# MLP matmuls with both activation parts side by side: one 512-column matmul in place of two of 256

## The chip, the cores and the metric

The kernel runs on one core of a Trainium2 chip. The metric is the device time of one execution in microseconds (us). Three runs of the kernel before gave 954.02, 955.78 and 957.56 us, median 955.78.

## The reference, cut to what matters

The reference is a small network on 256 tokens of width 1024 in float32: two transformer layers (attention, then an MLP), then an mLSTM mixer, an attention mixer with compressed and selected blocks, and a last norm. The change touches the two MLPs:

```python
def squared_relu_mlp(h, w_up, w_down):                 # w_up 1024 x 4096, w_down 4096 x 1024
    u = jnp.einsum("bsd,df->bsf", h, w_up)
    return jnp.einsum("bsf,fd->bsd", jnp.square(jax.nn.relu(u)), w_down)

h = rms_norm(x, g_mlp[layer])
x = x + squared_relu_mlp(h, w_up[layer], w_down[layer])
```

The norm's factor per token is taken out of the square: the kernel multiplies un-normed activations and scales the sum at the end.

## The kernel before, in words

Activations lie feature-major: a tile has 128 features on the partitions and the 256 tokens (`T`) as columns. Every matmul operand is cut into a high part (rounded to the reduced format `fp32r`) and a low part (what is left), and a product is the sum of three matmuls: high weights by high activations, high weights by low activations, low weights by high activations. The low-by-low product is left out.

Weights come as some 140 chunks of 128 x 2048 values, one DMA each on SyncE's queue (`prepare`, L120). ScalarE cuts the high part of a chunk in two halves (`whi`, L117), VectorE subtracts for the low part (`wlo`, L118). The ring has three buffers each of `wraw`, `whi` and `wlo`, so a chunk's buffers come free when TensorE has finished the chunk three before it.

`bank_add` (L189) issues, for every block of 128 input features and each of two output tiles (`j`), the three matmuls of 256 columns (L197, L199, L200), each with its own weight load. `gemm_feat` (L202) does that for one chunk: 8 blocks x 2 tiles x 3 = 48 matmuls into one PSUM bank (2 tiles x 256 columns). `gemm_tok` (L155) is the other form, used outside the MLPs: there the activations are the stationary operand and the weights stream, 512 columns at a time (L171 to L173).

`mlp` (L306): in the up part 16 chunks run, each giving 2 feature tiles of the hidden layer. ScalarE takes relu out of PSUM, VectorE squares, and both cut the square into `hh` and `hl` (`split`, L139). In the down part 4 groups of 4 chunks run; each group fills one bank, and `residual` (L278) scales it by the token's factor (`res`, L283), adds it to the stream `xT` (L285), and writes the next stage's operands `xh` (ScalarE, L237) and `xl` (VectorE, L238) and the squares for the norm. The two MLPs stand at about 116 to 287 us and 413 to 595 us of the span; the first is followed by `layer1`, whose first matmuls are of the 512-column form, the second by `mlstm`, whose first are `gemm_feat` chunks in an order written out by hand.

PSUM has eight banks: three for matmul outputs named `g`, two named `s` (attention scores, spare outputs), two `t`, one `o`. A scheduler orders each engine's instructions, mostly in the order of the program, and may pull a later chunk's matmuls forward where the next one would wait.

Of the kernel before, what the change touches and what calls it, by code (L numbers as in the profile page):

```python
# [8 lines left out]
F32 = mybir.dt.float32  # L9
F32R = mybir.dt.float32r  # L10
I32 = mybir.dt.int32
AF = mybir.ActivationFunctionType
ALU = mybir.AluOpType
# [3 lines left out]
P = 128  # L17
T = 256
KT = 8
# [48 lines left out]
def late(pool, shape, name):  # L68

    n = int(np.prod(shape))  # L70
    t = pool.tile([P, SHIFT + n], F32R, name=name, tag=name, bufs=1, align_bytes=LINE)[:, SHIFT:]
    names = "abcdefg"[:len(shape)]
    return t.rearrange(f"p ({' '.join(names)}) -> p {' '.join(names)}", **dict(zip(names, shape)))


class Builder:
# [229 lines left out]
    def mlp(self, gi_next):  # L306
        nc, tc = self.nc, self.tc
        with tc.tile_pool(name="mlp", bufs=2) as pool:
            hh = late(pool, [32, T], "hh")
            hl = late(pool, [32, T], "hl")  # L310
            for n in range(16):
                ps = self.gemm_feat()
                r = pool.tile([P, 2, T], F32, name="relu", tag="relu")
                s = pool.tile([P, 2, T], F32, name="rsq", tag="rsq")
                nc.scalar.activation(r, ps, AF.Relu)
                nc.vector.tensor_tensor(s, r, r, op=ALU.mult)
                self.split(hh[:, 2 * n:2 * n + 2], hl[:, 2 * n:2 * n + 2], s)
            self.norm_end("recip")
            row = self.rstd_row()
            if gi_next == 4:  # L320
                self.mlstm_fold()
            for n in range(4):
                b = self.bank()
                for c in range(4):
                    acts = [(hh[:, 8 * c + k], hl[:, 8 * c + k]) for k in range(8)]
                    self.bank_add(b, self.chunk(), 0, acts, c == 3)
                self.residual(2 * n, b["ps"], gi_next, row)


    def tok_evac(self, pool, ps, tag, sq=None, width=512, bufs=1):  # L330
# [805 lines left out]
    def build(self):  # L1136
        nc, tc = self.nc, self.tc
        with tc.tile_pool(name="keep", bufs=1) as keep, \
                tc.tile_pool(name="ring", bufs=3) as self.ring, \
                tc.tile_pool(name="small", bufs=2) as self.small, \  # L1140
                tc.tile_pool(name="pg", bufs=3, space=bass.MemoryType.PSUM) as self.pg, \
                tc.tile_pool(name="pa", bufs=1, space=bass.MemoryType.PSUM) as self.pa:
            self.vec = keep.tile([P, VEC.n], F32, name="vec", tag="vec")
            self.cst = keep.tile([P, CST.n], F32, name="cst", tag="cst")
            self.xT = keep.tile([P, KT, T], F32, name="xT", tag="xT")
            self.xh = late(keep, [KT, T], "xh")
            self.xl = late(keep, [KT, T], "xl")
            self.G = keep.tile([P, 16, 4], F32, name="G", tag="G")
            self.W8 = keep.tile([P, 2, 16, 8], F32, name="W8", tag="W8")
            self.ones = keep.tile([P, 1], F32, name="ones", tag="ones")  # L1150
            self.selr = keep.tile([P, 16], F32R, name="selr", tag="selr")
            nc.vector.memset(self.ones, 1.0)
            warm = keep.tile([P, 1], F32, name="warm", tag="warm")
            nc.scalar.activation(warm, self.ones, AF.Exp)
            self.ident = CST(self.cst, "ident")
            self.begin()
            self.pr = None
            with tc.tile_pool(name="p0", bufs=1, space=bass.MemoryType.PSUM) as self.p0:
                self.layer0()
            with tc.tile_pool(name="pr", bufs=2, space=bass.MemoryType.PSUM) as self.pr:  # L1160
                for s in (lambda: self.mlp(2), self.layer1, lambda: self.mlp(4), self.mlstm, self.nsa):
                    s()
# [146 lines left out]
```

## Time and profile before

| | |
|---|---|
| runs of the kernel before | 954.02, 955.78, 957.56 us (median 955.78) |
| the profiled execution's own time | 956.5 us |
| its span (first to last instruction) | 954.6 us |
| TensorE matmul busy | 936.7 us (98%) |
| weight load busy | 857.0 us (90%) |
| VectorE busy, ScalarE busy | 701.5 us (73%), 566.5 us (59%) |
| granted TensorE clock, mean | 0.997 |

Matmuls are pipelined: one row of a matmul lasts 0.28 us though the next begins 0.11 us later. So the pace of a stream of matmuls is read from the starts, or from how many stand in a stretch, not from the duration of one. A count in a stretch holds every matmul that touches it.

### The profile page before, as it was taken

The page shows a single profiled execution, that of the slowest core. Times are in us where ns is not written, and L with a number is a line of the kernel's source. Part 1 is how long each engine was busy: PE and PEld are TensorE (multiplying, and loading weights), DVE is VectorE, ACT ScalarE, POOL GpSimd, SP SyncE. Part 2 cuts the span into 40 slices and gives each one's busy share as a digit, 9 for nine tenths or more (in the row PEclk, how much of TensorE's full clock was granted, in tenths as well). Part 3 has the DMA queues.
Part 4 walks back from the last instruction along what each step waited for, and adds up shares of the span by engine and source line. Part 5 has one row for each costly group of instructions (what it writes and reads, how often), then busy time and mean ns, then how long its engine had stood idle before and what let it go on. Part 6 is the DMA issues. An engine that isn't in the chain of part 4 may idle for free.

```text
span 954.6 us, 17609 instructions
## 1 busy us (share of the span) xinstructions
PE 936.7 (98%) x7080; PEld 857.0 (90%) x7080; DVE 701.5 (73%) x1523; ACT 566.5 (59%) x1043; POOL 6.8 (1%) x16
## 2 busy tenths in 40 slices
PE   8998999999999999999999999999999999999997
PEld 5777899999998878899999999999888998988986
DVE  6788876664556887997665555978688877678994
ACT  7675665644435786765554344555755466379883
POOL 0000000000000000000000000000000000000000
PEclk9999999999999999999999999999999999999998
DMA  8823265555655333265555555544312555351311
GB/s 296 343 89 133 89 221 182 208 185 189 209 179 182 128 133 133 76 232 186 197 192 177 180 185 201 183 170 144 133 49 85 177 191 177 133 176 46 111 46 45
DMA packets 22610, 152.52 MB, mean 160 GB/s; under 512 B 2608, under 2 KB 2736, under 8 KB 4992
## 3 DMA queue, kind: packets, MB, share of 16 engines
q1 hardware_dynamic: 21744, 148.40, 45.1%
q0 software_dynamic: 784, 2.98, 0.9%
q8 instruction: 56, 0.92, 0.4%
q14 instruction: 26, 0.21, 0.1%
HBM read 150.33 MB, written 1.05 MB: 159 GB/s over the span
## 4 chain that ended last, share of the span: by engine, by line
PE 87%; ACT 5%; DVE 5%; issue 1%; DMA 1%; SPq 0%; ACTq 0%; DVEq 0%
PE g L197 19%; PE g L199 19%; PE g L200 18%; PE g L171 4%; PE g L173 4%; PE g L172 4%; PE o L475 2%; PE t L439 2%; DVE wlo L118 2%; ACT whi L117 2%; PE s L1043 1%; PE s L172 1%; PE s L171 1%; PE s L173 1%; PE t L366 1%; PE s L925 1%
## 5 line engine op out<-in xcount | busy, mean ns | idle before, releaser
L118 DVE TENSOR_TENSOR wlo<-wraw,whi 128x1024 fp32r<-128x1024 f32 (+1 forms) x274 | 325.3, 1204 | 143.9 <-ACT whi L117 143.4
L117 ACT ACTIVATE whi<-wraw 128x1024 fp32r<-128x1024 f32 (+1 forms) x274 | 277.5, 1042 | 228.8 <-PE g L199 121.8
L200 PE MATMUL g<-xh,wlo 128*128 128x256 f32 x928 | 261.4, 282 | 0.0
L199 PE MATMUL g<-xl,whi 128*128 128x256 f32 x928 | 260.4, 281 | 0.8 <-DVE xl L238 0.8
L197 PE MATMUL g<-xh,whi 128*128 128x256 f32 x928 | 260.5, 281 | 0.0
L197 PEld LDWEIGHTS g<-xh,whi 128*128 128x128 f32 x928 | 174.3, 188 | 3.7 <-issue 2.6
L199 PEld LDWEIGHTS g<-xl,whi 128*128 128x128 f32 x928 | 174.7, 188 | 1.5 <-DVE xl L238 1.2
L200 PEld LDWEIGHTS g<-xh,wlo 128*128 128x128 f32 x928 | 175.6, 189 | 0.5
L200 PE MATMUL g<-hh,wlo 128*128 128x256 f32 x512 | 142.9, 279 | 0.0
L197 PE MATMUL g<-hh,whi 128*128 128x256 f32 x512 | 142.9, 279 | 0.0
L199 PE MATMUL g<-hl,whi 128*128 128x256 f32 x512 | 142.8, 279 | 0.0
L199 PEld LDWEIGHTS g<-hl,whi 128*128 128x128 f32 x512 | 97.3, 190 | 0.0
L197 PEld LDWEIGHTS g<-hh,whi 128*128 128x128 f32 x512 | 96.2, 188 | 0.0
L200 PEld LDWEIGHTS g<-hh,wlo 128*128 128x128 f32 x512 | 96.2, 188 | 0.0
L171 PE MATMUL g<-whi,xh 128*128 128x512 f32 (+1 forms) x192 | 75.1, 391 | 0.9 <-ACT xh L237 0.9
L173 PE MATMUL g<-whi,xl 128*128 128x512 f32 (+1 forms) x192 | 74.2, 388 | 0.0
L172 PE MATMUL g<-wlo,xh 128*128 128x512 f32 (+1 forms) x192 | 74.0, 385 | 0.0
L197 PE MATMUL g<-yh,whi 128*128 128x256 f32 x224 | 62.7, 283 | 0.5 <-ACT yh L140 0.5
L199 PE MATMUL g<-yl,whi 128*128 128x256 f32 x224 | 62.6, 281 | 0.1
L200 PE MATMUL g<-yh,wlo 128*128 128x256 f32 x224 | 62.2, 280 | 0.0
L412 ACT ACTIVATE L<-L,nm 128x128 f32<-128x128 f32 (+1 forms) x128 | 56.9, 449 | 8.0 <-DVE nm L409 7.8
L171 PEld LDWEIGHTS g<-whi,xh 128*128 128x128 f32 x192 | 36.3, 189 | 10.6 <-ACT xh L237 2.9
(357 smaller groups left out, 1418.6 us busy)
## 6 DMA issues: line engine op xcount, KB each, us to landing
wraw<-in_w SPq DMA_DIRECT2D x135, 1024.0 KB, 5.0
wraw<-in_w SPq DMA_DIRECT2D x4, 512.0 KB, 7.8
tabs<-in_tabs SPq DMA_DIRECT2D x2, 1024.0 KB, 8.2
xT<-in_x SPq DMA_DIRECT2D x4, 256.0 KB, 7.9
bdv<-in_bdv POOLq DMA_DIRECT2D x8, 128.0 KB, 4.7
mlw<-in_mlw POOLq DMA_DIRECT2D x1, 992.0 KB, 5.2
nq<-in_gf POOLq DMA_DIRECT2D x1, 512.0 KB, 3.7
out_y<-nqr SPq DMA_DIRECT2D x2, 256.0 KB, 2.1
```

The costliest lines, as they stand in the source:

```text
L117: self.nc.scalar.activation(hi[:, s], w[:, s], AF.Copy)
L118: self.nc.vector.tensor_tensor(lo[:, s], w[:, s], hi[:, s].bitcast(F32), op=ALU.subtract)
L171: nc.tensor.matmul(ps[b][:, :n], xh, hi[:, sl], start=kt == 0, stop=False)
L172: nc.tensor.matmul(ps[b][:, :n], xh, lo[:, sl], start=False, stop=False)
L173: nc.tensor.matmul(ps[b][:, :n], xl, hi[:, sl], start=False, stop=kt == KT - 1)
L197: nc.tensor.matmul(o, hi[:, s], ah, start=bank["new"], stop=False)
L199: nc.tensor.matmul(o, hi[:, s], al, start=False, stop=False)
L200: nc.tensor.matmul(o, lo[:, s], ah, start=False, stop=last and j == 1 and i == len(acts) - 1)
L366: nc.tensor.transpose(ps[:, i, b * P:(b + 1) * P], t[:, b, c0 + i * P:c0 + (i + 1) * P], self.ident)
L412: nc.scalar.activation(Ls[i][:, c], Ls[i][:, c], AF.Exp, bias=nm[:, b, i:i + 1], scale=-1.0, accum_out=den[:, b, i:i + 1])
L439: nc.tensor.transpose(ps[:, e, j * P:(j + 1) * P], Ls[e][:, i * P:(i + 1) * P], self.ident)
L475: nc.tensor.matmul(o[64 * e:64 * e + 64, kt * P:T], v[:, kt, c0[e]:c0[e] + 64], pts[kt][:, e], start=start and kt == 0, stop=stop and kt == 1)
```

## The change

The low part of an activation is laid right behind its high part: `xx[:, k]` holds `xh` and `xl` of block `k` as 512 columns, `hx[:, f]` the same for the hidden layer. For each block and output tile there are now two matmuls in place of three: high weights by both parts (512 columns, one whole bank), and low weights by the high part (256 columns, the bank's first half). Each output tile has its own bank, one `g` and one `s`; the bank's two halves are added at the end by a ScalarE copy and a VectorE add per tile. Relu and square become one VectorE instruction on the sum.

```diff
-            hh = late(pool, [32, T], "hh")
-            hl = late(pool, [32, T], "hl")
+            hx = late(pool, [32, 2, T], "hx")
             for n in range(16):
-                ps = self.gemm_feat()
-                r = pool.tile([P, 2, T], F32, name="relu", tag="relu")
+                banks = self.wide()
+                self.wide_add(banks, self.chunk(), [self.xx[:, k] for k in range(8)], True, True)
+                u = self.wide_sum(pool, banks)
                 s = pool.tile([P, 2, T], F32, name="rsq", tag="rsq")
-                nc.scalar.activation(r, ps, AF.Relu)
-                nc.vector.tensor_tensor(s, r, r, op=ALU.mult)
-                self.split(hh[:, 2 * n:2 * n + 2], hl[:, 2 * n:2 * n + 2], s)
+                nc.vector.scalar_tensor_tensor(s, u, 0.0, u, op0=ALU.max, op1=ALU.mult)
+                self.split(hx[:, 2 * n:2 * n + 2, 0], hx[:, 2 * n:2 * n + 2, 1], s)
...
             for n in range(4):
-                b = self.bank()
+                banks = self.wide()
                 for c in range(4):
-                    acts = [(hh[:, 8 * c + k], hl[:, 8 * c + k]) for k in range(8)]
-                    self.bank_add(b, self.chunk(), 0, acts, c == 3)
-                self.residual(2 * n, b["ps"], gi_next, row)
+                    self.wide_add(banks, self.chunk(), [hx[:, 8 * c + k] for k in range(8)], c == 0, c == 3)
+                self.residual(2 * n, self.wide_sum(pool, banks), gi_next, row)
+
+    def wide(self):
+        return [self.pg.tile([P, 2, T], F32, name="g", tag="g"), self.single("s", [P, 2, T])]
+
+    def wide_add(self, banks, w, acts, first, last):
+        nc = self.nc
+        hi, lo = w
+        for i, a in enumerate(acts):
+            for j in range(2):
+                s = slice((2 * i + j) * P, (2 * i + j + 1) * P)
+                nc.tensor.matmul(banks[j], hi[:, s], a, start=first and i == 0, stop=False)
+                nc.tensor.matmul(banks[j][:, 0], lo[:, s], a[:, 0], start=False, stop=last and i == len(acts) - 1)
+
+    def wide_sum(self, pool, banks):
+        u = pool.tile([P, 2, T], F32, name="wsum", tag="wsum")
+        for j in range(2):
+            self.nc.scalar.activation(u[:, j], banks[j][:, 1], AF.Copy)
+            self.nc.vector.tensor_tensor(u[:, j], banks[j][:, 0], u[:, j], op=ALU.add)
+        return u
...
-            self.xh = late(keep, [KT, T], "xh")
-            self.xl = late(keep, [KT, T], "xl")
+            self.xx = late(keep, [KT, 2, T], "xx")
+            self.xh, self.xl = self.xx[:, :, 0], self.xx[:, :, 1]
```

The program's order is changed by this at three places that matter below. On TensorE, the first matmuls of the first MLP stand so before (`g_1332` is the bank of the first chunk):

```order
L197 MATMUL g_1332<-xh_73,whi_1165 128x256 [waits DVE_49,Activation_49]
L199 MATMUL g_1332<-xl_74,whi_1165 128x256 [waits DVE_49]
L200 MATMUL g_1332<-xh_73,wlo_1166 128x256
L197 MATMUL g_1332<-xh_73,whi_1165 128x256
L199 MATMUL g_1332<-xl_74,whi_1165 128x256
L200 MATMUL g_1332<-xh_73,wlo_1166 128x256
```

and so now:

```order
L338 MATMUL g_1330<-xx_73,whi_1164 128x512 [waits DVE_49,PE_49]
L339 MATMUL g_1330<-xx_73,wlo_1165 128x256
L338 MATMUL s_1331<-xx_73,whi_1164 128x512
L339 MATMUL s_1331<-xx_73,wlo_1165 128x256
L338 MATMUL g_1330<-xx_73,whi_1164 128x512 [waits DVE_49]
```

The first matmul of a block waited for ScalarE's high part alone; now it waits for VectorE's low part as well. Both streams have the same number of columns per block.

On VectorE, one chunk in the middle of the first MLP's up part stood so before (cut of the weights, square, cut, low part of the hidden layer):

```order
L118 TENSOR_TENSOR wlo_2216<-wraw_2217,whi_2215 128x1024 [waits DMAHW7_49,PE_49,Activation_49]
L316 TENSOR_TENSOR rsq_2209<-relu_2208 128x512 [waits Activation_49]
L118 TENSOR_TENSOR wlo_2216<-wraw_2217,whi_2215 128x1024 [waits Activation_49]
L141 TENSOR_TENSOR hl_1331<-rsq_2209,hh_1330 128x512 [waits Activation_49]
L118 TENSOR_TENSOR wlo_2279<-wraw_2280,whi_2278 128x1024 [waits DMAHW0_49,PE_49,Activation_49]
```

and so now:

```order
L345 TENSOR_TENSOR wsum_2086<-g_2044,wsum_2086 128x256 [waits Activation_49]
L118 TENSOR_TENSOR wlo_2098<-wraw_2099,whi_2097 128x1024 [waits DMAHW0_49,PE_49,Activation_49]
L345 TENSOR_TENSOR wsum_2086<-s_2045,wsum_2086 128x256 [waits Activation_49]
L118 TENSOR_TENSOR wlo_2098<-wraw_2099,whi_2097 128x1024 [waits Activation_49]
L315 SCALAR_TENSOR_TENSOR rsq_2091<-wsum_2086 128x512 [waits DVE_49]
L141 TENSOR_TENSOR hx_1329<-rsq_2091,hx_1329 128x2x256 [waits Activation_49]
```

Two adds are new, and the square stands behind both cuts.

At the end of the second MLP VectorE's order was, from the last cuts in the MLP to the first instructions of `mlstm` (`cw`, `cb`, `gsb` belong to `mlstm`):

```order
L283 TENSOR_TENSOR res<-g,row 128x512
L647 TENSOR_SCALAR cw<-vec 128x64
L648 TENSOR_SCALAR cb<-vec 128x16
L285 TENSOR_TENSOR xT<-res,xT 128x512
L657 MEMSET gsb 128x256
L118 TENSOR_TENSOR wlo<-wraw,whi 128x1024
L238 SCALAR_TENSOR_TENSOR xl<-xT,vec,xh 128x256 x2
```

and is now:

```order
L345 TENSOR_TENSOR wsum<-g,wsum 128x256
L118 TENSOR_TENSOR wlo<-wraw,whi 128x1024
L345 TENSOR_TENSOR wsum<-s,wsum 128x256
L118 TENSOR_TENSOR wlo<-wraw,whi 128x1024
L283 TENSOR_TENSOR res<-wsum,row 128x512
L285 TENSOR_TENSOR xT<-res,xT 128x512
L666 TENSOR_SCALAR cw<-vec 128x64
L667 TENSOR_SCALAR cb<-vec 128x16
L676 MEMSET gsb 128x256
L690 MEMSET xi 128x2x3 x2
L238 SCALAR_TENSOR_TENSOR xx<-xT,vec,xx 128x256 x2
```

Both cuts of a chunk now stand ahead of the residual; ScalarE's order there has the same shape (copy, cut, copy, cut, then `xx`).

## Rows read from the trace of the kernel before

**Rows 1.** The page: busy time by engine, and the chain by engine.

```profile
PE 936.7 (98%) x7080; PEld 857.0 (90%) x7080; DVE 701.5 (73%) x1523; ACT 566.5 (59%) x1043; POOL 6.8 (1%) x16
...
PE 87%; ACT 5%; DVE 5%; issue 1%; DMA 1%; SPq 0%; ACTq 0%; DVEq 0%
```

**Rows 2.** The page's groups: first matmul of each triple of 256 columns.

```profile
L197 PE MATMUL g<-xh,whi 128*128 128x256 f32 x928 | 260.5, 281 | 0.0
...
L197 PE MATMUL g<-yh,whi 128*128 128x256 f32 x224 | 62.7, 283 | 0.5 <-ACT yh L140 0.5
```

**Rows 3.** TensorE by windows: length, busy (matmuls touching it), granted clock, DMA.

```profile
125.00:195.00 70.00, 70.00 (x620) 1.00 0.58 200
205.00:285.00 80.00, 80.00 (x708) 1.00 0.57 197
430.00:500.00 70.00, 70.00 (x597) 1.00 0.56 192
510.00:590.00 80.00, 80.00 (x681) 1.00 0.54 188
```

**Rows 4.** Timeline of TensorE in `layer1`, 512-column stream after a break at 298.1.

```profile
299.02 0.40 PE L173 MATMUL s<-whi,xl 128*128 128x512 f32 x1
...
300.18 0.39 PE L172 MATMUL s<-wlo,xh 128*128 128x512 f32 x1
...
302.00 0.39 PE L171 MATMUL s<-whi,xh 128*128 128x512 f32 x1
...
308.12 0.39 PE L171 MATMUL s<-whi,xh 128*128 128x512 f32 x1
```

**Rows 5.** Timeline of TensorE, 256-column streams at two breaks.

```profile
416.76 0.39 PE L197 MATMUL g<-xh,whi 128*128 128x256 f32 x2
417.62 0.39 PE L199 MATMUL g<-xl,whi 128*128 128x256 f32 x1 [0.47 <-DVE xl L238]
...
595.07 0.28 PE L197 MATMUL g<-xh,whi 128*128 128x256 f32 x1
...
602.02 0.28 PE L200 MATMUL g<-xh,wlo 128*128 128x256 f32 x1
...
602.94 0.28 PE L197 MATMUL g<-xh,whi 128*128 128x256 f32 x1
...
606.80 0.28 PE L199 MATMUL g<-xl,whi 128*128 128x256 f32 x1
```

**Rows 6.** Timeline of ScalarE and VectorE, one chunk of the first up part.

```profile
161.26 1.06 ACT L117 ACTIVATE whi<-wraw 128x1024 fp32r<-128x1024 f32 x1 [1.85 <-PE g L199]
...
164.22 0.63 ACT L140 ACTIVATE hh<-rsq 128x512 fp32r<-128x512 f32 x1 [0.46 <-DVE rsq L316]
...
162.36 1.22 DVE L118 TENSOR_TENSOR wlo<-wraw,whi 128x1024 fp32r<-128x1024 f32 x1 [1.88 <-ACT whi L117]
...
165.24 0.68 DVE L141 TENSOR_TENSOR hl<-rsq,hh 128x512 fp32r<-128x512 f32 x1
```

**Rows 7.** Timeline of ScalarE and VectorE, end of the second MLP.

```profile
595.15 2.01 ACT L117 ACTIVATE whi<-wraw 128x1024 fp32r<-128x1024 f32 x2 [3.59 <-PE g L199]
597.06 0.90 ACT L237 ACTIVATE xh<-xT,vec 128x256 fp32r<-128x256 f32 x2
...
595.27 0.69 DVE L283 TENSOR_TENSOR res<-g,row 128x512 f32<-128x512 f32 x1 [2.27 <-PE g L200]
...
596.05 0.68 DVE L285 TENSOR_TENSOR xT<-res,xT 128x512 f32<-128x512 f32 x1
...
598.01 0.87 DVE L238 SCALAR_TENSOR_TENSOR xl<-xT,vec,xh 128x256 fp32r<-128x256 f32 x2
```

**Rows 8.** By line: 256-column copy out of PSUM, 256-column add (ns min/median/max).

```profile
L275 ACT ACTIVATE row<-t x5: 362/384/401, 200.9 to 810.1; 128x256 f32<-128x256 f32 x5
...
L250 DVE TENSOR_TENSOR acc<-acc,sq x42: 406/416/427, 8.4 to 787.9; 128x256 f32<-128x256 f32 x42
```

## The prediction

> **What bounds the kernel now.** I read the page first: TensorE is busy for 98% of the span and makes 87% of the chain that ended last [rows 1]. Matmul rows overlap, so the share says only that nothing else is in the way for long; what a stage costs is the pace of its starts. I took that from windows inside the two MLPs. A window counts every matmul that touches it, some 2.4 more than start in it (0.28 us over 0.114). First MLP: 620 in 70 us and 708 in 80 us, so 150 us / (1328 - 4.9) = 113.4 ns from start to start. Second MLP: 597 and 681, so 150 / (1278 - 4.8) = 117.8 ns [rows 3]. There is no gap in either (busy for the whole window), the granted clock is 1.00 in all four, the 2.4 GHz level, and the code is the same. So one stream of 256-column matmuls has two paces, and the second MLP runs at the slower one from end to end.
>
> Where does a pace begin? At a break. TensorE waits at 416.76 to 417.62 for the last blocks of `xh` and `xl`, and from there on the second MLP is slow. From 595.07 to 602.02 there are 59 matmuls in 6.95 us (117.8 ns); then four tiny norm matmuls break the stream, and from 602.94 to 606.80 there are 34 in 3.86 us (113.5 ns) [rows 5]. A stream of 256 columns keeps what it fell into until the next break.
>
> A stream of 512 columns doesn't. After a break at 298.1 it runs at 1.16 us for 5 matmuls (232 ns) between 299.02 and 300.18, and from 302.00 to 308.12 there are 27 in 6.12 us: 226.7 ns, twice 113.4 [rows 4]. It comes to the quick pace by itself within some 3 us.
>
> **The change part by part.**
>
> *Streams.* An MLP has 32 chunks of 16 (block, tile) pairs, 512 in all. A pair was three matmuls of 256 columns: 3 x 113.4 = 340 ns in the first MLP, 3 x 117.8 = 353.4 ns in the second. Now it is one of 512 and one of 256: 226.7 + 113.4 = 340 ns at the quick pace. The columns are the same, 768, and a 512-column matmul costs exactly two of 256, so the 1024 matmuls and weight loads that go are worth nothing by themselves. What can be won is the slow pace. No row shows 512 and 256 columns in turn. The bounds are 340 ns (quick) and 353.4 ns (slow) in each MLP. I take 340 in both, since two thirds of the columns now flow in matmuls of the kind that comes back by itself. First MLP 0 (bounds 0 and 512 x 13.4 ns = +6.9 us), second MLP -6.9 us (bounds -6.9 and 0).
>
> The Trainium skill ("TensorE: Matmul & The Clock Gate", section "Wait — 56ns, not 53.3ns?") gives a matmul at the full clock N / 2.4 plus a fixed 2.5 ns or so, whatever N is. By that, 1024 matmuls fewer are worth an estimated 2.6 us more. The rows differ: with a fixed part a 512-column matmul would take less than two of 256, and it takes 226.7 against 2 x 113.4.
>
> *The way into the up part.* The first matmul of a block now also waits for the low part, while before, TensorE streamed the high part (one matmul, 0.11 us) during that wait [rows 5]. +0.1 us for each MLP, +0.2 (bounds 0 and +0.4: two late blocks each).
>
> *Evacuation in the up part.* Per chunk ScalarE gets two copies of 256 columns (0.38 each) in place of a relu, VectorE two adds (0.42 each) [rows 8]; the square stays one instruction of 512 columns, taken as 0.68 like the low part [rows 6]. VectorE is then busy 2 x 1.22 + 2 x 0.42 + 2 x 0.68 = 4.6 of 5.44 us per chunk. The work also forms a ring over both engines: copy 0.38, cut 1.06, cut 1.22 on VectorE, add 0.42, cut 1.22, square 0.68, high part 0.63, then the next copy: 5.61 us, less about 0.08 at each of the four steps that stay on an engine (two cuts in a row take 2.01, not 2.12 [rows 7]), plus 0.03 at each of the three crossings: 5.4 us. That fits into 5.44, barely. Cover if it doesn't: only two `s` banks, so chunk n+2 waits for the add of chunk n, which ends some 2.9 us after the chunk's last matmul, 2.5 us before it is needed. I take 0 (bounds 0 and +3.4, the rival below).
>
> *The end of the second MLP.* This is the step that costs. Before, `res` began at 595.27, 0.3 us after the last matmul of the MLP, and the two `xl` were ready at about 598.5 and at 598.88 [rows 7]. `mlstm` needs its seventh block 36 matmuls after 595.07: 599.15 to 599.3. Cover 0.7 us. Now, with the last matmul at the same 594.95: copy of the `g` bank 594.93 to 595.31, cut to 596.3, copy of `s` to 596.6, cut to 597.55 on ScalarE; on VectorE add to 595.8, cut 596.33 to 597.55, add to 597.9, cut to 599.0, `res` to 599.65, `xT` to 600.25. Then `xh` of the seventh block (0.50) at 600.8 and its `xl` at 601.3. TensorE waits from 599.15 to 600.8, does one matmul, and waits 0.4 us more for `xl`: +2.0 us. Bounds: +0.6, if only the copy and the two adds came on top (1.2 us, less the cover of the present order), and +2.7, if each of the new instructions took 0.1 us longer.
>
> *The end of the first MLP* has the same later residual, but `layer1` begins with 36 matmuls of 512 columns ahead of the seventh block, 36 x 0.227 = 8.2 us after the MLP's end, and its operand is ready after 6.3: nothing. If that cover went, the same 2 us would come in.
>
> *Breaks inside the new streams.* Each costs a few matmuls at 232 instead of 227 ns, 0.06 us; three per MLP, +0.2.
>
> *Streams elsewhere.* 928 + 224 triples, less the 512 of the up parts, are 640 triples of 256 columns outside the MLPs [rows 2], 13.4 ns each between the two paces, 8.6 us in all. Their code is unchanged, but every break before them shifts, and each may fall the other way: 0, give or take 1.5.
>
> Sum: 0 - 6.9 + 0.2 + 0 + 2.0 + 0 + 0.2 = -4.5. The profiled execution took 956.5 us (span 954.6 and 1.9 around it), so 952.0 for one like it. It stands 0.7 above the median of the runs, 955.8, and the forecast for a median is 951.3.
>
> **The rivals.**
>
> *A pace that stays slow in both MLPs* (slower than before). If the 256-column matmul between two of 512 keeps the slow pace locked, and both MLPs fall into it at their first wait, the first loses 6.9 us and the second wins nothing: 955.8 + 6.9 + 2.4 = 965.1. For it: the first MLP could lose what it has by luck, and each weight load of a 512-column matmul still has only a 256-column one to hide behind. Against it: rows 4. The point from which the change loses: (p - 340) x 1024 = 6.9 - 2.4, a pair of 344.4 ns.
>
> *The pace belongs to the place, not to the stream.* Before, four timed or profiled executions lie within 3.6 us of each other, less than one MLP's 6.9, so the second MLP may be slow each time for a reason of its own. Then 340 and 353.4 stay as they are, and the new costs remain: 955.8 + 2.4 = 958.2. Against it: the stream in front of the break at 416.76 uses the same tiles, and the pace turned at 602.13 without any change of tiles.
>
> *The ring of ScalarE and VectorE is longer than a chunk.* At 5.7 us instead of 5.4, the lag grows by 0.26 us a chunk, 4.2 over 16, and the 2.5 us of cover are gone in the last third: TensorE waits 1.7 us in each MLP, 951.3 + 3.4 = 954.7. For it: the margin is 0.04 us. Against it: it needs each new instruction to be slower than its rows.
>
> *A fixed part per matmul after all*, as on the skill's page: 951.3 - 2.6 = 948.7. Stated as a mechanism of this kernel: both streams would show less than 340 ns a pair. Rows 3 and 4 speak against it.
>
> **How the numbers follow.** Forecast 0.57 (its own range 949 to 954, from the end of the second MLP and the streams elsewhere), both slow 0.13, pace of the place 0.14, ring 0.10, fixed part 0.06. Half a per cent, 4.8 us, is about what a measurement of this kernel can tell from no change: faster is below 951.0, slower above 960.6. The forecast's middle lies 0.3 us above the first bound, so 0.24 of its 0.57 counts as faster; with the fixed part 0.30. Slower: both slow 0.13, and 0.01 from the edge of the pace of the place. Same: 0.56. The range 948.7 to 960.8 leaves out both slow and some 0.06 of the forecast's lower end.
>
> **What would show it.** In windows inside both MLPs, pairs of 340 ns (in 70 us, 2 matmuls per pair: about 412 starts); 353 in one of them proves a rival. At the end of the second MLP a wait of TensorE on L197 for `xx` from ScalarE of 1.5 to 1.7 us and one of 0.4 on VectorE. In the up part ScalarE's first copy of a chunk starting at the same distance from the chunk's last matmul in chunk 3 and in chunk 15; if it drifts, the ring is too long. I am wrong if the second MLP's pace doesn't change, or if the first's does.

## The result and the profile after

The changed kernel takes 965.97 us (median of 6 runs, 962.62 to 968.05) against 954.93 for the kernel before beside it (953.45 to 960.50). The ratio is 1.0099, interval 1.0074 to 1.0125: slower by 1%, where the forecast was 951.3 with a range up to 960.8. It is the first rival almost to the number: "a pace that stays slow in both MLPs", 965.1.

The page of the changed kernel, busy time and chain, to stand beside [rows 1]:

```profile
PE 943.3 (98%) x6056; PEld 816.1 (85%) x6056; DVE 734.7 (76%) x1603; ACT 572.7 (60%) x1091; POOL 6.8 (1%) x16
...
PE 86%; DVE 7%; ACT 5%; issue 1%; DMA 1%; SPq 0%; ACTq 0%; DVEq 0%
```

1024 matmuls are gone (7080 to 6056), and TensorE is busy 6.6 us longer. Where, the windows of [rows 3] tell, now of the changed kernel (length, busy and matmuls touching it, granted clock, DMA share, GB/s):

```profile
125.00:195.00 70.00, 70.00 (x399) 1.00 0.54 191
205.00:285.00 80.00, 80.00 (x455) 1.00 0.53 185
430.00:500.00 70.00, 70.00 (x398) 1.00 0.55 194
510.00:590.00 80.00, 80.00 (x456) 1.00 0.52 181
```

No gap, and the granted clock is 1.00, as before. Some 1.9 of a window's matmuls only touch it, so the first MLP has (854 - 3.8) / 2 = 425 pairs in 150 us, 353 ns each, and the second the same. By the starts themselves it is 353.3 in all four parts, 13.3 above the 340 that the forecast took. The way into the first up part, in the timeline of TensorE, shows how soon the pace is there:

```profile
110.10 0.28 PE L200 MATMUL g<-yh,wlo 128*128 128x256 f32 x1
110.22 0.39 PE L338 MATMUL g<-xx,whi 128*128 128x512 f32 x1
110.44 0.28 PE L339 MATMUL g<-xx,wlo 128*128 128x256 f32 x1
110.56 0.40 PE L338 MATMUL s<-xx,whi 128*128 128x512 f32 x1
110.79 0.28 PE L339 MATMUL s<-xx,wlo 128*128 128x256 f32 x1
110.91 0.40 PE L338 MATMUL g<-xx,whi 128*128 128x512 f32 x1
```

The stream in front runs at the quick pace (109.88 to 110.22 is three matmuls of 113). The first 512 columns still take 0.22 us, the 256 after them 0.12, and from the second pair on it is 0.35 for a pair.

By the first and last matmul of each stage, in us:

| stage | before | after | difference |
|---|---|---|---|
| to the first up part | 111.4 | 110.2 | -1.2 |
| first MLP | 175.7 | 182.0 | +6.3 |
| `layer1` | 125.6 | 125.6 | 0 |
| second MLP | 182.3 | 182.1 | -0.2 |
| behind it, to the last matmul | 352.4 | 354.1 | +1.7 |

The sum is +6.7 before rounding, the difference of the two profiled executions (962.77 against 956.5) +6.3. The medians are 11.0 apart: the profiled execution of the changed kernel lies 3.2 us below its median (its six runs stand in the order of their mean granted clock, from 962.62 us at 0.999 to 968.05 at 0.994), and that of the kernel before 1.6 above its own.

The wait at the end of the second MLP, forecast as 1.65 us on `xh` and 0.4 on `xl`, in the waits of TensorE (engine, line, waited for: us, times, longest):

```profile
PE g L197 <- ACT xx L237: 1.4, 1, 1.4
```

and in its timeline:

```profile
604.19 0.28 PE L200 MATMUL g<-xx,wlo 128*128 128x256 f32 x1
605.90 0.38 PE L197 MATMUL g<-xx,whi 128*128 128x256 f32 x1 [1.42 <-ACT xx L237]
606.42 0.39 PE L199 MATMUL g<-xx,whi 128*128 128x256 f32 x1
```

By the starts the two matmuls come 1.71 and 0.52 us behind the one before, where the pace is 0.12: 1.6 and 0.4 us are lost, as forecast. The view of the waits counts only the 1.4 us in which the engine is idle.

ScalarE and VectorE there, where [rows 7] stood:

```profile
600.20 1.05 ACT L117 ACTIVATE whi<-wraw 128x1024 fp32r<-128x1024 f32 x1
601.15 0.38 ACT L344 ACTIVATE wsum<-s 128x256 f32<-128x256 f32 x1
...
602.76 1.21 DVE L118 TENSOR_TENSOR wlo<-wraw,whi 128x1024 fp32r<-128x1024 f32 x1
603.89 0.68 DVE L283 TENSOR_TENSOR res<-wsum,row 128x512 f32<-128x512 f32 x1
```

The last matmul starts at 599.95, so `res` comes 3.9 us behind it (0.3 before), each sum behind a cut of weights, in the order that was forecast.

The evacuation in the up part, by line from 125 to 195 us (busy, mean ns), beside [rows 6, 8]:

```profile
L344 ACT ACTIVATE wsum<-g 128x256 f32<-128x256 f32 x12 | 4.6, 386 | 5.0 <-PE g L339 5.0
...
L315 DVE SCALAR_TENSOR_TENSOR rsq<-wsum 128x512 f32<-128x512 f32 x13 | 8.9, 685 | 0.0
L345 DVE TENSOR_TENSOR wsum<-g,wsum 128x256 f32<-128x256 f32 x12 | 5.1, 424 | 0.1
```

386, 424 and 685 ns, against 384, 416 and 680 taken. TensorE waits nowhere for it.

### The profile page after: what moved, and what is told of

Same layout as the page of the kernel before. It is cut to its first block, busy times and chain, and to the rows that moved or that the text cites. A ratio compares the mean times of both kernels' runs of the same rounds, so it can differ in the third digit from the quotient of the medians.

```text
span 961.0 us, 15652 instructions
## 1 busy us (share of the span) xinstructions
PE 943.3 (98%) x6056; PEld 816.1 (85%) x6056; DVE 734.7 (76%) x1603; ACT 572.7 (60%) x1091; POOL 6.8 (1%) x16
## 4 chain that ended last, share of the span: by engine, by line
PE 86%; DVE 7%; ACT 5%; issue 1%; DMA 1%; SPq 0%; ACTq 0%; DVEq 0%
PE g L338 12%; PE s L338 12%; PE g L197 6%; PE g L199 6%; PE s L339 6%; PE g L339 6%; PE g L200 6%; PE g L171 4%; PE g L173 4%; PE g L172 4%; PE o L494 2%; DVE wlo L118 2%; PE t L458 2%; ACT whi L117 1%; PE s L1062 1%
## 5 line engine op out<-in xcount | busy, mean ns | idle before, releaser
L197 PE MATMUL g<-xx,whi 128*128 128x256 f32 x416 | 118.1, 284 | 1.4 <-ACT xx L237 1.4
L200 PE MATMUL g<-xx,wlo 128*128 128x256 f32 x416 | 118.5, 285 | 0.0
L199 PE MATMUL g<-xx,whi 128*128 128x256 f32 x416 | 117.4, 282 | 0.1
L338 PE MATMUL g<-xx,whi 128*128 128x512 f32 x256 | 101.7, 398 | 0.3 <-DVE xx L238 0.2
L338 PE MATMUL g<-hx,whi 128*128 128x512 f32 x256 | 101.9, 398 | 0.0
L338 PE MATMUL s<-hx,whi 128*128 128x512 f32 x256 | 101.7, 397 | 0.0
L338 PE MATMUL s<-xx,whi 128*128 128x512 f32 x256 | 101.6, 397 | 0.0
L197 PEld LDWEIGHTS g<-xx,whi 128*128 128x128 f32 x416 | 78.3, 188 | 5.4 <-issue 3.0
L199 PEld LDWEIGHTS g<-xx,whi 128*128 128x128 f32 x416 | 78.4, 188 | 0.7 <-DVE xx L238 0.3
L200 PEld LDWEIGHTS g<-xx,wlo 128*128 128x128 f32 x416 | 78.3, 188 | 0.5
L171 PE MATMUL g<-whi,xx 128*128 128x512 f32 (+1 forms) x192 | 75.2, 391 | 0.1
L172 PE MATMUL g<-wlo,xx 128*128 128x512 f32 (+1 forms) x192 | 74.1, 386 | 0.0
L173 PE MATMUL g<-whi,xx 128*128 128x512 f32 (+1 forms) x192 | 74.0, 386 | 0.0
L339 PE MATMUL g<-xx,wlo 128*128 128x256 f32 x256 | 71.9, 281 | 0.0
```

Source lines behind the costliest of these rows:

```text
L171: nc.tensor.matmul(ps[b][:, :n], xh, hi[:, sl], start=kt == 0, stop=False)
L172: nc.tensor.matmul(ps[b][:, :n], xh, lo[:, sl], start=False, stop=False)
L173: nc.tensor.matmul(ps[b][:, :n], xl, hi[:, sl], start=False, stop=kt == KT - 1)
L197: nc.tensor.matmul(o, hi[:, s], ah, start=bank["new"], stop=False)
L199: nc.tensor.matmul(o, hi[:, s], al, start=False, stop=False)
L200: nc.tensor.matmul(o, lo[:, s], ah, start=False, stop=last and j == 1 and i == len(acts) - 1)
```

## The experiments

All times are medians. A ratio, with its 95% interval, is to the kernel before, run beside it on the same chip; a kernel that was run once has none. "Part" is the up or the down part of one MLP: 16 chunks of 16 pairs. Paces are from the starts of the matmuls in the trace.

**Is it the layout, or the width?** The high part's 512 columns cut in two, with the layout, the two banks and the sum as changed:

```diff
-nc.tensor.matmul(banks[j], hi[:, s], a, ...)
+nc.tensor.matmul(banks[j][:, 0], hi[:, s], a[:, 0], ...)
+nc.tensor.matmul(banks[j][:, 1], hi[:, s], a[:, 1], ...)
```

> The changed kernel with its layout, its two banks per chunk and its sum at the end, but each pair as three matmuls of 256 columns again. Mix (two widths in turn hold the stream at the slow pace): the four long stretches (up and down of both MLPs) can run at 340 ns per pair again, at least some of them; time 952 to 962 us, by how many do. Layout (two banks in turn, or low part behind high part, make the slow pace): all four stay at 353 ns, time about 965. Draw (each break draws a pace at random, and the changed kernel drew slow four times): some at 340, some at 353.

963.1 us (ratio 1.0071, 1.0046 to 1.0097). Windows as above:

```profile
125.00:195.00 70.00, 70.00 (x597) 1.00 0.57 199
205.00:285.00 80.00, 80.00 (x681) 1.00 0.52 183
430.00:500.00 70.00, 70.00 (x620) 1.00 0.58 205
510.00:590.00 80.00, 80.00 (x682) 1.00 0.53 182
```

597, 681 and 682 are the counts of the slow MLP in [rows 3], 620 that of the quick one: 353.3 ns in three parts, 340.0 in one. So layout, banks and sum allow the quick pace, and it belongs to a part, not to the kernel. Two or three matmuls per pair take the same 353.3.

**Fewer changes of width.** Per chunk sixteen matmuls of 512 columns, then sixteen of 256:

```diff
+for part in range(2):
     for i, a in enumerate(acts):
         for j in range(2):
-            matmul(banks[j], hi ...); matmul(banks[j][:, 0], lo ...)
+            if part == 0: matmul(banks[j], hi ...)
+            else: matmul(banks[j][:, 0], lo ...)
```

> The changed kernel with each chunk's matmuls in another order: first the 16 of 512 columns, then the 16 of 256. Mix: the 512s come back to 226.7 ns within a few matmuls, the 256s after them keep that pace: 5.44 us a chunk, time 951 to 953 us. Layout: the 512s stay at 235 ns, 5.65 us a chunk, time about 965. Draw: as many chunks at either pace as the breaks give, the 512s quick, the 256s either.

957.27 us (ratio 0.9995, 0.9979 to 1.0011); 346.7 ns per pair in all four parts, apart from the first one to three chunks of each, where matmuls change places. The timeline of one chunk splits it:

```profile
129.15 0.40 PE L340 MATMUL s<-xx,whi 128*128 128x512 f32 x1
...
132.42 0.40 PE L340 MATMUL s<-xx,whi 128*128 128x512 f32 x1
...
133.00 0.28 PE L342 MATMUL s<-xx,wlo 128*128 128x256 f32 x1
...
134.36 0.28 PE L342 MATMUL s<-xx,wlo 128*128 128x256 f32 x1
```

Fourteen matmuls of 512 columns from 129.15 to 132.42 are 233.6 ns each, twelve of 256 from 133.00 to 134.36 are 113.3. The 256s are quick, the 512s never come to 226.7. That is not what any of the theories had said.

**Many ways in.** One small fp32 matmul (a nick) ahead of every chunk, in the changed kernel and in the one before:

```diff
+def nick(self):
+    ps = self.pa.tile([P, 512], F32, name="t", tag="t", bufs=PSUM["t"])
+    self.nc.tensor.matmul(ps[:, :1], self.ident, self.ones, start=True, stop=True)
```

> The changed kernel with one matmul of a single column ahead of each of the 64 MLP chunks, a break of some 0.1 to 0.2 us each (64 of them: +7 to +14 us by themselves). Mix and layout: all 64 chunks run at 353 ns per pair. Draw: each chunk draws anew, and a good part of the 64 run at 340 ns.

> The kernel before with the same single-column matmul ahead of each of its 64 MLP chunks. Draw: chunks of three 256-column matmuls at 340 and at 353 ns, mixed within one MLP. If the pace is set by the place (first MLP quick, second slow), all of the first MLP at 340 and all of the second at 353.

977.05 us (1.0215, 1.0187 to 1.0243) and 967.31 us (1.0117, 1.0085 to 1.0149). The first chunk of each up part also waits for its operands and is left out. In the changed kernel the other 62 are at 353.3; in the kernel before they are at 113.4 ns per matmul behind the nick, in the second MLP too. From its timeline, where 42 matmuls in 4.76 us make 113.3:

```profile
437.44 0.28 PE L334 MATMUL t<-ones,cst 128*128 128x1 f32 x2
...
438.13 0.28 PE L199 MATMUL g<-xl,whi 128*128 128x256 f32 x1
...
442.89 0.28 PE L199 MATMUL g<-xl,whi 128*128 128x256 f32 x1
```

So the pace is not drawn by chance at each break: the same way in gave the same pace 62 times. A nick costs 0.25 us there.

**Banks.** The loops exchanged, so that the bank changes every 16 matmuls; and the same in the grouped form:

```diff
-for i, a in enumerate(acts):
-    for j in range(2):
+for j in range(2):
+    for i, a in enumerate(acts):
```

> The changed kernel with its two loops exchanged: for each chunk eight pairs (512 columns high, 256 low) on one PSUM bank, then eight on the other, so that the bank changes every 16 matmuls instead of every second. Width theory (a stream in which 512 and 256 columns take turns is held at the slow pace whatever the bank): 353.3 ns per pair in all four stretches, 963 to 966 us. Bank theory (the bank that changes at every second matmul holds it): the stream comes to 340 ns per pair a few matmuls after each change of bank, about 340 to 343 over a chunk, 951 to 954 us.

> The grouped kernel with the bank outermost: per chunk and bank eight matmuls of 512 columns, then eight of 256. In the grouped kernel before it the sixteen 512-column matmuls, whose bank changes at each, stood at 236 and 231 ns in turn and never came to 226.7, while the sixteen of 256 columns on the same two banks stood at 113.4. Bank theory: without the change of bank the 512s come to 226.7 within a few, so 341 to 344 ns per pair, 951 to 955 us. Width theory (the step from 256 to 512 columns disturbs, and the disturbance decays over five to ten 512-column matmuls as after any other break): eight are too few, so the 512s keep a mean of 231 to 234 ns, 344 to 347 per pair, 955 to 958 us.

965.83 us (1.0101, 1.0056 to 1.0147) with 353.3 in all parts, and 957.57 (1.0018, 0.9987 to 1.0048) with 346.7, its 512s again at 236 and 231 in turn. The bank has no part in it.

**One width.** The low weights through both activation parts, `banks[j], lo[:, s], a`:

> The changed kernel with the low weights' matmul widened to both activation parts, so that every matmul of the MLPs is 512 columns (this adds the product of the two low parts, and 1024 columns flow per pair instead of 768). Width theory: one width alone, so each stream comes to 226.7 ns per matmul after some ten matmuls, as the 512-column streams outside the MLPs do, 453.3 ns per pair; time 966 + 1024 x 0.1 = 1068 us. Bank theory: two banks in turn hold it slow, 233 to 235.5 ns per matmul, 467 to 471 per pair; 1082 to 1086 us. Draw (each break draws a pace that stays): some stretches 453.3, some 471.

1079.11 us. The timeline, 128 matmuls apart:

```profile
150.29 0.40 PE L338 MATMUL s<-xx,whi 128*128 128x512 f32 x1
...
180.16 0.40 PE L338 MATMUL s<-xx,whi 128*128 128x512 f32 x1
```

29.87 us / 128 = 233.4 ns, and it stays there in all four parts. So a stream of nothing but 512 columns does not come to 226.7 either. That falsifies the width theory, and the banks are out already. What is left between these 512s and those of [rows 4]: there the weights move and the activations are stationary, and the tiles lie otherwise. `late` (lines 68 to 73) lays activations 192 bytes behind a 256-byte line; `chunk_tiles` (lines 111 to 113) lays weights at 192 where they move and at 0 where they are stationary, as in the MLPs.

**A single nick per part**, in the kernel before (`if n == 1` in the up part, `if n == 0 and c == 1` in the down part):

> The kernel before with four single-column fp32 matmuls in all: one ahead of the second feature tile pair of the up part and one ahead of the second chunk of the down part, in each MLP. With one ahead of every chunk, all 64 chunks of the kernel before stood at 113.4 ns per 256 columns behind it, and a nick cost 247 ns. Entry theory (the way in sets the pace until the next break): the second MLP goes from 353.4 to 340 ns per pair over about 480 pairs, -6.4 us, four nicks +1.0: about 5.4 us faster than before if before's second MLP is slow in most runs. Place theory (the second MLP is slow for another reason, and the nick must come back at each chunk): no gain, +1.0 us.

953.1 us against 955.64 (0.9973, 0.9947 to 0.9999), 2.5 us less where 5.4 were expected if the second MLP is slow in most runs. Behind the nicks all four parts are at 340.0; the first chunk of each down part, ahead of its nick, is at 353.3. The third nick was issued ahead of an attention matmul of `layer1` instead of in the up part, so the second up part came in quick by itself. This kernel is the fastest version of this study, by 0.3%.

**Where the operands lie.** In the changed kernel and in the all-512 form the weights' offset steps by 32 bytes every two chunks; in a third kernel each quarter of `hx` has an offset of its own:

```diff
-at = SHIFT if self.chunk_no in TOK else 0
+at = SHIFT if self.chunk_no in TOK else 8 * (self.chunk_no // 2 % 8)
```

> The changed kernel with the weights' parts laid, for every two chunks, 32 bytes further into their 256-byte line (offsets 0, 32, ... 224 bytes, then again), where the kernel lays those of the MLPs at 0 and the activations at 192. Width theory (512 and 256 columns in turn are slow wherever they lie): 353.3 ns per pair in all chunks, 966 us. Offset theory (the pace depends on where stationary and moving operands begin within their lines; the 512-column streams outside the MLPs, which settle at 226.7 ns, have both at 192): the pace changes from chunk pair to chunk pair, and comes to 340 at some offset, likely 192.

> The changed kernel with the hidden activations of the down parts laid at other offsets within their 256-byte line, one for each quarter: 0, 64, 128 and 192 bytes in the first MLP, 32, 96, 160 and 224 in the second (192 everywhere in the changed kernel); up parts as they were. Width theory: 353.3 ns per pair in all chunks. Offset theory: the down parts' chunks change pace with a period of four chunks, 340 at some offset and 353 or more at others, the up parts stay at 353.3.

> The kernel with all matmuls of the MLPs at 512 columns (it adds the product of the low parts), with the weights' offset stepped by 32 bytes every two chunks. At offset 0 every one of its matmuls took 233.3 ns, 466.7 per pair, with no second width in the stream, and 512-column streams outside the MLPs take 226.7. Offset theory: 453.3 ns per pair at some offsets, likely 192, and 466.7 or more at others. Operand theory (512 columns of activations through stationary weights take 233.3 wherever they lie): 466.7 in all chunks.

966.13, 966.51 and 1080.3 us, one execution each. Mixed stream, weights at 0 bytes (the first two rows, 16 pairs apart) and at 160 (the last two, 16 pairs):

```profile
134.19 0.40 PE L338 MATMUL g<-xx,whi 128*128 128x512 f32 x1
...
139.84 0.40 PE L338 MATMUL g<-xx,whi 128*128 128x512 f32 x1
...
190.13 0.39 PE L338 MATMUL g<-xx,whi 128*128 128x512 f32 x1
...
195.68 0.40 PE L338 MATMUL g<-xx,whi 128*128 128x512 f32 x1
```

5.65 / 16 = 353.1 ns against 5.55 / 16 = 346.9. In ns per pair (mean of two chunks, each by its last eight pairs), the same within 1 ns in all four parts but for the mixed stream at 192, which showed two values:

| weights at byte | 0 | 32 | 64 | 96 | 128 | 160 | 192 | 224 |
|---|---|---|---|---|---|---|---|---|
| mixed | 353.3 | 346.9 | 351.4 | 350.0 | 348.9 | 346.7 | 346.7 or 354 | 353.2 |
| all 512 | 466.7 | 468.5 | 465.2 | 466.7 | 458.2 | 466.2 | 453.4 | 466.7 |

With the activations' offset the mixed stream's down parts went between 346.7 (32 and 160 bytes) and 353.8 (0). And at 192 bytes, where both operands lie as in [rows 4], the all-512 stream is quick (nine pairs in 4.08 us, 453.3 each):

```profile
344.89 0.39 PE L338 MATMUL g<-hx,whi 128*128 128x512 f32 x1
...
348.97 0.39 PE L338 MATMUL s<-hx,whi 128*128 128x512 f32 x1
```

So the pace hangs on where both operands begin in their 256-byte lines. ScalarE and VectorE write the weights at the same offset, but they are done with a chunk well ahead (in the all-512 form 211.3 us for the chunk that is multiplied from 222.5), and the pace changes with the chunk that TensorE reads. The 512s of `layer1` need no other reason for being quick than their offsets.

**Both parts of the weights apart.** 8 x 8 offsets of high and low part, one pair for each of the 64 chunks, in the changed kernel and in the one before:

```diff
+at = (8 * (i % 8), 8 * (i // 8))        # i: the chunk's number among the 64
```

> The changed kernel with an offset of its own for the weights' high and for their low part, another pair of offsets (steps of 32 bytes, 8 x 8) in each of the 64 chunks of the MLPs; the activations stay at 192 bytes. With both parts stepped together the pairs took 346.6 to 354.0 ns, the same at the same offset in all four parts. Offset theory, a matmul's pace is set by its own moving operand and the weights that are loaded beside it: some of the 64 pairs of offsets come to 340 to 343 ns, since the two kinds of matmul can be set apart. Width theory (two widths in turn cost at least 6.6 ns per pair wherever they lie): no pair of offsets under 346.

> The kernel before (256 columns only) with the same 64 pairs of offsets, one for each chunk of its MLPs. Offset theory: its two paces, 340 and 353.3 ns per triple at offset 0 and 0, become one or other (or values between) by the offsets, whatever the chunk before had, and some pairs of offsets give 340. Draw theory (only the way into a stream decides and the offset has no part): one pace, 340 or 353.3, from each break to the next, through all offsets.

963.52 and 966.64 us. Two chunks of each hold a break. Of the changed kernel's other 62 (by the second half of each), 61 lie at 346.4 to 353.8 ns; with the high part at 0 and the low part at 192 it is 340.2. So the mixed stream can run at the quick pace. In the kernel before they lie at 346.4 to 363.2, at more levels than its two, so the offsets act on one width as well.

**That one address** in the whole of both MLPs (`wlo` at 192 bytes, `whi` at 0), in the changed kernel and in the one before:

> The changed kernel with one address moved: in the MLPs the low part of the weights begins 192 bytes into its line, as the activations do, and the high part stays at 0. In the sweep this was the only one of 63 readable pairs of offsets at which the mixed stream came to 226.7 ns per 512 and 113.4 per 256 columns, 340.2 ns per pair. Offset theory: all four parts come to 340 a few pairs behind each break and stay, 1024 pairs x 13.3 ns = 13.6 us less than the changed kernel's 966.0: 952.4 us, some 2.5 to 4 us faster than the kernel before. Width theory (the sweep's one chunk was a lucky way in, not the offset): 353.3 in some or all of the four parts, 959 to 966 us.

> The kernel before with the same address moved: in the MLPs the weights' low part at 192 bytes, the high part at 0. In the sweep of the kernel before this pair of offsets gave 353.8 ns per triple. Offset theory: the pace is a matter of each operand's offset, so here all four parts stand near 353.8 where the kernel before had 340 in the first MLP, 512 triples x 13.4 ns = 6.9 us slower than before, 962 to 964 us. Draw theory (offsets have no part in a stream of one width): some parts at 340, 955 to 958 us.

960.84 us (956.97 to 967.13; 1.0044, 1.0012 to 1.0076) and 968.59 (1.0123, 1.0082 to 1.0164). Windows of the first:

```profile
125.00:195.00 70.00, 70.00 (x402) 1.00 0.56 195
205.00:285.00 80.00, 80.00 (x459) 1.00 0.53 185
430.00:500.00 70.00, 70.00 (x413) 1.00 0.54 195
510.00:590.00 80.00, 80.00 (x459) 1.00 0.53 187
```

350.0, 350.0, 340.0 and 350.0 ns. The offset theory got half: the quick pace is there now, in one part of four, and not in the part where the sweep had shown it. In the kernel before the same address does harm: 353.4, 366.7, 353.4, 353.4. So offsets set which paces a stream may have, and something else picks among them.

**The way in, at these offsets.** A nick of 1, 2, 4 ... 128 columns ahead of each chunk, single in eight chunks, double in the next eight:

```diff
+w = 1 << k % 8
+for _ in range(1 + k // 8 % 2):
+    self.nc.tensor.matmul(ps[:, :w], self.ident, self.ident[:, :w], start=True, stop=True)
```

> The changed kernel with the low part of the weights at 192 bytes and a small fp32 matmul ahead of every chunk of the MLPs, of 1, 2, 4, ... 128 columns in turn, one of it or (in every other eight chunks) two. At these offsets the mixed stream stood at 350.0 ns per pair in three parts and at 340.0 in the fourth. Entry theory (at given offsets a stream has a few paces that last, and the way in picks one): chunks with the same nick have the same pace, 340 behind some widths and 350 behind others. Rival (the pace drifts by itself): 340 and 350 without regard to the width.

983.6 us, one execution. Behind a double nick of 2, 8 or 128 columns the chunk is at 340 in all four parts, behind one of 1, 4, 16, 32 or 64 at 350 in all four: 32 chunks without an exception. Singles settle less: the same width gave 350 in one part and 353.4 in another, and the two first chunks of the down parts (one column, among other small matmuls) are at 340. Each width always stood at the same place of its part, so this run alone can't tell the two apart; the next has the double of two columns at other places. The timeline behind a double of 2 (14 pairs from 167.24) and of 4 (14 pairs from 173.13):

```profile
166.44 0.50 PE L334 MATMUL t<-cst 128*128 128x2 f32 x4
...
167.24 0.39 PE L348 MATMUL s<-xx,whi 128*128 128x512 f32 x1
...
172.00 0.39 PE L348 MATMUL s<-xx,whi 128*128 128x512 f32 x1
...
172.34 0.50 PE L334 MATMUL t<-cst 128*128 128x4 f32 x4
...
173.13 0.40 PE L348 MATMUL s<-xx,whi 128*128 128x512 f32 x1
...
178.03 0.39 PE L348 MATMUL s<-xx,whi 128*128 128x512 f32 x1
```

4.76 / 14 = 340 ns, and 4.90 / 14 = 350. With two columns more in each small matmul, every pair of the chunk behind it takes 10 ns more.

**The quick way in, once per part**, the double nick of two columns at four places:

> The changed kernel with the weights' low part at 192 bytes and a pair of two-column fp32 matmuls at four places: ahead of the third chunk of each up part and of the second chunk of each down part. In the sweep of small matmuls the pair of two columns was followed by 340.4 ns per pair in four chunks of four. Entry theory: 928 of the 1024 pairs at 340.0 in place of 353.3, 928 x 13.3 ns = 12.3 us less than the changed kernel, four nicks of 0.44 us more: 966.0 - 12.3 + 1.8 = 955.5 us, level with the kernel before. Rival (the quick pace lasts a chunk, as in the sweep, and falls back later): some parts return to 350, 957 to 961 us.

956.5 us against 956.83 (0.999, 0.9953 to 1.0028). Windows:

```profile
125.00:195.00 70.00, 70.00 (x414) 1.00 0.57 199
205.00:285.00 80.00, 80.00 (x473) 1.00 0.55 196
430.00:500.00 70.00, 70.00 (x398) 1.00 0.52 187
510.00:590.00 80.00, 80.00 (x474) 1.00 0.56 195
```

Three parts are at 340.0 from the nick to their end. The third stays at 353.4, as it was ahead of the nick, where the other three had 350: the way in seems to include the stream in front, though this is one case. So the pace lasts through a part, and with three parts quick the changed kernel is level with the kernel before: the change's loss is the slow pace.

**The kernel before, once more:**

> The kernel before, unchanged, for a second profile of it. In the first its first MLP stood at 340 ns per triple and its second at 353.4. Entry theory with entries that differ from run to run: another pattern of 340 and 353.3 over the four parts, and a span that follows it, 954.6 us less or plus 3.4 us for every part that changes pace (256 triples x 13.4 ns). Rival (the program fixes the entries): 340, 340, 353.4, 353.4 again, within 1 us of 954.6.

951.89 us, and 963.71 for another execution of the same kernel beside it, without a profile (its mean granted clock was the higher one, 0.999 against 0.995, so the clock doesn't explain it). The windows of the first:

```profile
125.00:195.00 70.00, 70.00 (x620) 1.00 0.57 199
205.00:285.00 80.00, 80.00 (x709) 1.00 0.55 195
430.00:500.00 70.00, 70.00 (x620) 1.00 0.57 196
510.00:590.00 80.00, 80.00 (x709) 1.00 0.55 189
```

All four parts are quick: 597 and 681 of [rows 3] have become 620 and 709. So the slow second MLP is not there in every execution. The span is 950.1, 4.5 below 954.6: the second MLP gives 6.6, and 1.5 ahead of the first MLP and 0.6 behind the second go the other way. The 1.5 are lost where the granted clock is 0.52 from 91.00 to 98.00 us, mostly at the 1.2 GHz level; it is 1.00 there in the first profile.

## Why the prediction was wrong

*The streams* failed, and with them the sum. The prediction put it: "I take 340 in both, since two thirds of the columns now flow in matmuls of the kind that comes back by itself." It is 353.3 in both, the upper bound: 6.3 us more in the first MLP and nothing won in the second. Between the two profiled executions the sum was -4.5 and the stages give +6.7, 11.2 apart. The two MLPs are 12.6 off, +6.3 where +0.2 stood and -0.2 where -6.7 stood; 1.2 ahead of the first MLP and 0.3 behind the second go the other way. The inference behind it was that the 512s of [rows 4] are quick because they are 512 wide. They differed from the new ones in a second thing, the offset of the weights in their line (192 bytes against 0), and that was it: at offset 0 a stream of 512s alone stands at 233.4 ns, at 192 it stands at 226.7.

*A pace kept from break to break* was right, in both kernels. Wrong was to take the slow second MLP of one profiled execution as a loss of every run, which the change could win back. In the second profile there is none, so in a median run only a share of the 6.9 us was there to win. Against a run with four quick parts the changed kernel's slow pairs come to an estimated 1024 x 13.3 = 13.6 us. Measured, 962.77 against 951.89, it is 10.9: 12.8 in the two MLPs and 0.8 behind them, less 2.7 ahead of the first, where the quick run lost time to its clock (the last experiment).

*The rival of a pace that stays slow in both MLPs* had the outcome and the size: 965.1 and "a pair of 344.4 ns" as the point from which it decides; 353.3 is beyond. That 965.1 is so near is partly luck, since its sum, too, took the second MLP of the kernel before as slow in a median run. Its reason was half right. The slow pace is locked with every way in that was tried at these offsets, but not because of the 256 columns between: in the grouped order and in one width the 512s don't come to 226.7 either. Its chance, 0.13, was too low, since one example stood for a law.

*The pace belongs to the place* (958.2): fell with the second profile of the kernel before.

*The ring* of ScalarE and VectorE fits, as forecast. With 5.65 us for a chunk it had room; in the run with the double nicks a chunk takes 5.44 us and TensorE is busy all 70.00 and 80.00 us of the windows.

*A fixed part per matmul* fell: 353.3 ns with two matmuls per pair and with three, 340.0 with two and with three. The Trainium skill ("TensorE: Matmul & The Clock Gate", section "Wait — 56ns, not 53.3ns?") gives a fixed 2.5 ns or so for each matmul; no run here shows it, and what a matmul takes above its columns went by the offsets.

*The end of the second MLP*: right in kind, order and size, by the starts 1.6 us for `xh` and 0.4 for `xl` where 1.65 and 0.4 were forecast. *The way into the up part*: the wrong sign, though small. By the starts the late block costs 0.37 and 0.46 us in the two MLPs, 0.49 and 0.63 before, so -0.3 in all where +0.2 was taken. *Streams elsewhere*: `layer1` 0, the part ahead of the first MLP -1.2, what lies behind the wait -0.3, inside the 1.5.

## What to carry to other kernels

When one program shows two paces at the same clock and without a gap, compare every property of the quick and the slow stream, addresses within a line among them, before one of them (here the width) is called the cause; and take a second profile before a slow stretch is booked as a gain. A sweep of the offset, one value for each chunk of a long loop, reads a whole table from a single execution; but a value from one chunk must be tried in the whole loop, as the 340.2 here held in one part of four. What a change of form is worth can then be asked at the best offsets seen of both forms: here it was nothing, 340 ns per pair in either.

## What the runs showed of the hardware

- At a granted clock of 1.00, a matmul's time per column took several lasting values: 226.7, 233.4 and 235 ns for 512 columns, 113.4 and 117.8 for 256, up to a mean of 122 in a triple (366.7).
- Which of them a stream may have hangs on where the stationary and the moving operand begin within 256 bytes; at given offsets the matmuls in front have a part in picking one, and it stays until the next break (up to a whole part of 16 chunks). Two columns more in each of two small matmuls moved the next pairs by 10 ns each.
- At the offsets of the changed kernel its stream of 512 and 256 columns in turn only ever settled at 353.3; in other orders the same columns took 346.7 (grouped) and 340.0 or 353.3 (three matmuls of 256). With the low weights at 192 bytes 340.0, 350.0 and 353.4.
- What in the chip makes an offset slow stays open. The trace shows no wait in these streams, and the weight loads take 187 to 193 ns each: 187.8 on average at the quick pace of the kernel before, 189.3 at its slow one, 187.8 in the changed kernel's. Why the entries of the kernel before differ from run to run was not tried either.
